# Merging all four token tiles' fetched expert results on VectorE inside the last unit, instead of two on VectorE and two by identity products

## The chip, the core and the metric

One core of one Trainium2 chip runs the whole program. TensorE (PE in the rows) does the matrix products, VectorE (DVE) and ScalarE (ACT) the elementwise work, GpSimd (POOL) a few small operations and the issuing of some transfers, SyncE (SP) the issuing of the weight loads. The metric is the device time of one execution in microseconds; lower is better.

## What is computed

Two trunk layers over 256 context tokens and 256 latent tokens of width 1024. The part that matters here is the seam between the two layers: the mixture of experts of layer 0 ends, its result is added to the stream, and layer 1 begins with its normalisation and its key and value projection. Cut from the reference:

```
comb = jnp.sum(jax.nn.one_hot(global_idx, N_EXPERTS, dtype=F32) * w_exp[..., None], axis=1)
for e in range(N_EXPERTS):
    he = jax.nn.silu(t @ w1[e]) * (t @ w3[e])
    out = out + comb[:, e:e + 1] * (he @ w2[e]).astype(F32)
xl = xl + g2l * hier_moe(hl2, ...)          # the same for the context stream with g2c
...
hl = modulate(rmsnorm(xl, norm1[1]), sh1l, sc1l)      # layer 1 begins
q, k, v = _split(h @ w_qkv, QKV_SPLITS)
```

Each token has two experts. All 512 tokens are four tiles of 128: tiles 0 and 1 are context, 2 and 3 are latent.

## The kernel before

**Units.** Layer 0's experts run as `NU = 12` units (the loop from line 1881, `e` is the place in the order `SEQ`). A unit multiplies its gathered tokens by w1 and w3 (`hidden`), forms `he` = silu times the other product on VectorE (line 1894), turns `he` on TensorE, copies it with ScalarE, and multiplies by w2 into two PSUM banks `py` (lines 1913 to 1928). The first ten units scale `py` and scatter the rows into a memory table `yd`, one half of it for each of a token's two experts. The last two units (`N_LAST = 2`) don't go through memory: ScalarE and VectorE split the scaled `py` into a high part `yh` and a low part `yl` (lines 1947 and 1948, both named `yl` in the rows), and one-hot products with `back` bring them into token order (`to_tokens`, line 1958).

**The fetch.** At the start of unit 10, `get_parts` (line 1859) issues eight loads of 512 KB from GpSimd, two for each tile in the order 0, 1, 2, 3: what the first ten units left in `yd`. Tiles 0 and 1 land in `parts_p` (`pt` in the rows, both of a tile), tiles 2 and 3 in two `d4` tiles each (`ya`, `yb`). The loads can start only when the scatter of unit 9 has landed.

**Two ways into the stream.** `merge(t)` (line 1869) is four VectorE instructions: add the two fetched tiles, multiply by the gate `g2` in two halves, add to the residual `xres`. It runs for tiles 0 and 1, in unit 11, after the products that turn `he`. For tiles 2 and 3, `to_tokens` instead adds the fetched tiles to its PSUM sum by products with the identity: two for each half tile, eight in all (lines 1966 and 1967). After the loop, `finish_half(t, n)` (line 1969) gates the PSUM sum and adds it to `xres` on VectorE and squares on ScalarE; `sums` and `normal` make the normalised tile; `turned` (line 2001) transposes on TensorE; `columns1` (line 2010) applies the modulation on VectorE and splits into two parts; `kv_split` splits the key and value weights.

**What sets the order.** `pin(...)` makes the named engines keep the order of the program text: `m1` from unit 10 on pins TensorE and VectorE, and `fin` (line 2021) pins VectorE, ScalarE and TensorE. So in unit 11 VectorE runs `he`, `merge(0)`, `merge(1)`, then the two `yl`, and an instruction that waits for a load holds all that stand behind it. After the loop TensorE runs `to_tokens` of tiles 0 and 1, one adaLN step (`ada_go`), `to_tokens(2)`, the first transposes `turned((0, 1), 0)`, `to_tokens(3)`, and then the other transposes; the key and value products follow.

**Weights** arrive through SyncE's queue in a ring of slots that the consuming engines free.

Of the kernel before, what the change touches and what calls it, by code (L numbers as in the profile page):

```python
# [27 lines left out]
NU = 12  # L28
# [82 lines left out]
N_LAST = 2  # L111
# [27 lines left out]
def backbone(ctx, tc, I, out):  # L139
    nc = tc.nc  # L140
    act, dve, pool, pe, sp = (Pinned(tc, e) for e in (nc.scalar, nc.vector, nc.gpsimd, nc.tensor, nc.sync))

    def pin(where):
        names = PIN.get(where, "")
        for e, nm in ((act, "a"), (dve, "d"), (pool, "g"), (pe, "p"), (sp, "s")):
            e.on = nm in names
# [11 lines left out]
    def acc():  # L158
        return acc_p.tile([P, 512], F32, tag="acc", name="acc")

    def aux():
        return aux_p.tile([P, 512], F32, tag="aux", name="aux")
# [68 lines left out]
    def feed(key):  # L231
        state["fed"] = where[key]
        pump(state["fed"] + len(slots))
        return loaded.pop(key)
# [125 lines left out]
    ident = const.tile([P, P], F32, name="ident")  # L360
# [193 lines left out]
    def high_if(x):  # L554
        return tc.high_priority() if x else ExitStack()
# [857 lines left out]
    for kk in range(2):  # L1413
        for c in range(4):
            k = 2 * c + kk
# [53 lines left out]
    for n in range(4):  # L1469
        ps = aux()  # L1470
# [6 lines left out]
    for d in range(2):  # L1477
        seq = list(range(8)) if d == 0 else [3, 2, 1, 0, 7, 6, 5, 4]
        for ct in range(2):
            n4 = 2 * d + ct  # L1480
            dsb = [aux(), aux()]
            for c in seq[:-1]:
                pr, t = c % 2, c // 2
# [39 lines left out]
    for tpr in range(2):  # L1523
        at = {}
        for d in range(2):
            ps = [aux(), aux()]
# [25 lines left out]
        ps = [aux(), aux()]  # L1552
        for ti in range(2):
            t = 2 * tpr + ti
            for ct in range(2):
                reg = slice((2 * ti + ct) * P, (2 * ti + ct + 1) * P)
                for pr in range(2):
                    h = 2 * ct + pr
                    for d in range(2 - AT_SUM):
                        pe.matmul(ps[pr][:, reg], at[d, pr][:, reg], vt[:, t, h * P:(h + 1) * P],  # L1560
                                  start=(d == 0), stop=False)
# [8 lines left out]
        for pr in range(2):  # L1570
            o, jk = ob[:, 2 * tpr + pr, :], tmp("jk")
            act.activation(o, ps[pr], AF.Copy)
            for ti in range(2):
                for ct in range(2):
                    reg = slice((2 * ti + ct) * P, (2 * ti + ct + 1) * P)
                    n = (2 * tpr + ti) * 4 + 2 * ct + pr
# [5 lines left out]
    for t in range(4):  # L1582
        for h in range(4):
            n = 4 * t + h
# [24 lines left out]
    for b in range(4):  # L1609
        ps = aux()  # L1610
# [71 lines left out]
    def d4(name):  # L1682
        return wk.tile([P, D], F32, tag="d4", name=name, bufs=N_D4)
# [9 lines left out]
    def fetch_x(i):  # L1693
        if i < NU:
            if i < 2:
                xg = xgs[i] = xg01[:, i * D:(i + 1) * D]
            else:
                xg = xgs[i] = d4("xg")
            if 2 <= i < N_D4:
                pool.memset(xg, 0.0)  # L1700
            gather(0, xg, ix[:, SEQ[i]:SEQ[i] + 1])
# [152 lines left out]
    parts = {}  # L1854
# [14 lines left out]
    def merge(t):  # L1869

        ya, yb = parts[t]
        dve.tensor_tensor(ya, ya, yb, op=ALU.add)
        for n in range(2):
            sl = slice(n * 512, (n + 1) * 512)
            dve.tensor_tensor(ya[:, sl], ya[:, sl], g2[int(t < 2)][n], op=ALU.mult)
        dve.tensor_tensor(xres[:, t, :], xres[:, t, :], ya, op=ALU.add)
# [4 lines left out]
    for e in range(NU):  # L1881
        two = SEQ[e] >= BIG
        if AHEAD > 2:
            fetch_x(e + AHEAD)
        if e == NU - N_LAST:
            pin("m1")
            get_parts()
        sl = wk.tile([P, 512], F32, tag="sl", name="sl")
        act.activation(sl, hs[e, 0], AF.Silu)
        hidden(e, 1, 0)  # L1890
        hidden(e, 1, 1)
        he = wk.tile([P, 4, P], F32, tag="he", name="he")
        with high_if(HE):
            dve.tensor_tensor(he.rearrange("q k p -> q p k"), sl.rearrange("q (p k) -> q p k", k=4),
                              hs[e, 1].rearrange("q (p k) -> q p k", k=4), op=ALU.mult)
        if e + 1 < NU:
            hidden(e + 1, 0, 0)
        ps = aux()
        for k in range(4):
            pe.transpose(ps[:, k * P:(k + 1) * P], he[:, k, :], ident)  # L1900
        hh = wk.tile([P, 512], F32 if two else F32R, tag="hh", name="hf" if two else "hh")
        if not two:
            hl = wk.tile([P, 512], F32R, tag="hl", name="hl")
        with high_if(HE):
            act.activation(hh, ps, AF.Copy)
            if not two:
                dve.tensor_tensor(hl, ps, hh.bitcast(F32), op=ALU.subtract)
        if e + 1 < NU:
            hidden(e + 1, 0, 1)
        if e == NU - 1:  # L1910
            for t in range(2):
                merge(t)
        py = [acc(), acc()]
        for h in range(2):
            if two:
                raws = [feed((2, 0, e, o, h)) for o in range(2)]
                for n in range(2):
                    for kk in range(2):
                        k = 2 * h + kk
                        halves(py[n], hh[:, k * P:(k + 1) * P], raws,  # L1920
                               slice(kk * D + n * 512, kk * D + (n + 1) * 512), k == 0, k == 3)
            else:
                for q, wh, wl in quarters(e, 2, h):
                    k = 2 * h + q
                    ks = slice(k * P, (k + 1) * P)
                    for n in range(2):
                        ws = slice(n * 512, (n + 1) * 512)
                        mm3(py[n], (hh[:, ks], hl[:, ks]), (wh[:, ws], wl[:, ws]), k == 0, k == 3)
            if h == 0 and e + 2 < NU:
                prep_x(e + 2)  # L1930
        if e == NU - LESS:
            less_slots(parts_p)
        if e == 1:
            last_ow = d4("ow")
            for n in range(N_LAST):
                last_tokens(NU - 1 - n)
            A1B1 = ada_cols(1)
        if e == 2:
            for n in range(N_LAST):
                turn_last(NU - 1 - n)  # L1940
        if e == 4:
            g2 = [rows_pe(rowt, i, 2, mod[0], 2) for i in range(2)]
        if e >= NU - N_LAST:
            yh, yl = last_y[e] = [wk.tile([P, D], F32R, tag="d4", name="yl", bufs=N_D4) for _ in range(2)]
            for n in range(2):
                sl = slice(n * 512, (n + 1) * 512)
                act.activation(yh[:, sl], py[n], AF.Copy, scale=wgt[:, SEQ[e]:SEQ[e] + 1])
                dve.scalar_tensor_tensor(yl[:, sl], py[n], wgt[:, SEQ[e]:SEQ[e] + 1], yh[:, sl].bitcast(F32),
                                         op0=ALU.mult, op1=ALU.subtract)
        else:  # L1950
            y = d4("y")
            for n in range(2):
                act.activation(y[:, n * 512:(n + 1) * 512], py[n], AF.Copy, scale=wgt[:, SEQ[e]:SEQ[e] + 1])
            scatter(0, ix[:, NU + SEQ[e]:NU + SEQ[e] + 1], y)
# [3 lines left out]
    def to_tokens(t, n):  # L1958

        sl = slice(n * 512, (n + 1) * 512)  # L1960
        ps = fin[t, n] = (acc, aux)[n]()
        for e in range(NU - N_LAST, NU):
            for k in range(2):
                pe.matmul(ps, back[e - NU][:, t * P:(t + 1) * P], last_y[e][k][:, sl],
                          start=(e + k == NU - N_LAST), stop=(t < 2 and e + k == NU))
        for k in range(2 if t >= 2 else 0):
            pe.matmul(ps, ident, parts[t][k][:, sl], start=False, stop=(k == 1))

    def finish_half(t, n):
        sl = slice(n * 512, (n + 1) * 512)  # L1970
# [30 lines left out]
    def turned(tiles, k2):  # L2001

        ps = aux()
        for k in (k2, k2 + 1):
            for n, t in enumerate(tiles):
                c = 256 * (k - k2) + n * P
                pe.transpose(ps[:, c:c + P], xn[t][:, k * P:(k + 1) * P], ident)
        return ps

    def columns1(s, tiles, k2, ps, v_of):  # L2010

        for k in (k2, k2 + 1):
            v = v_of()
            dve.tensor_scalar(v, ps[:, 256 * (k - k2):256 * (k - k2) + 256], A1[:, k, s:s + 1],
                              B1[:, k, s:s + 1], op0=ALU.mult, op1=ALU.add)
            for n, t in enumerate(tiles):
                hi, lo = (x[t][:, k, :] for x in hs1)
                act.activation(hi, v[:, n * P:(n + 1) * P], AF.Copy)
                dve.tensor_tensor(lo, v[:, n * P:(n + 1) * P], hi.bitcast(F32), op=ALU.subtract)
# [33 lines left out]
    kv_split(0, 0)  # L2053
    ps = [turned((0, 1), 0)]
    v1 = lambda: wk.tile([P, 256], F32, tag="v", name="v", bufs=N_V)
    for n in range(2):
        to_tokens(3, n)
    sums(2, 1)
    for k2 in range(0, KD, 2):
        if k2:  # L2060
            ps.append(turned((0, 1), k2))
        columns1(1, (0, 1), k2, ps.pop(0), v1)
        if k2 < 6:
            kv_split((k2 + 2) // 4, (k2 + 2) // 2 % 2)
        if k2 == 2:
            finish_half(3, 0)
            finish_half(3, 1)
# [403 lines left out]
    for p in range(NE // 2):  # L2471
# [12 lines left out]
        sl, he = (wk.tile([P, 512], F32, tag="y", name=nm, bufs=4) for nm in ("sl", "he"))  # L2484
# [22 lines left out]
        for h in range(2):  # L2507
            raws = [feed((2, 1, 2 * p + o, h)) for o in range(2)]
            for i in range(4):
                n, kk = (i % 2, i // 2) if p >= NE // 2 - KKM else (i // 2, i % 2)  # L2510
                k = 2 * h + kk
# [21 lines left out]
    for n in range(2):  # L2533
        for t in range(2):
            sl = slice(n * 512, (n + 1) * 512)
# [103 lines left out]
```

## Time and profile before

| | us |
|---|---|
| median of 3 executions | 984.44 (983.81 to 985.03) |
| the profiled execution, whole | 992.14 |
| its span | 990.3 |
| TensorE busy in the span | 903.5 (91%) |
| VectorE busy | 528.2 (53%) |
| ScalarE busy | 399.7 (40%) |
| GpSimd busy | 120.8 (12%) |

All stamps below are microseconds from the start of the span of that one profiled execution. TensorE's share is an average over stages with different limits; the seam between the layers lies at about 577 to 645 us. A matmul's end is modelled by the profile, so the starts are what to go by.

### The profile page before, as it was taken

The numbers are of one execution on the slowest core, as the hardware profiler recorded it, in microseconds if no ns is written. First come the engines' busy times: TensorE is split into PE (matmuls) and PEld (weight loads), VectorE is DVE, ScalarE is ACT, GpSimd is POOL, SyncE is SP. The second block draws the span as 40 slices with busy tenths as digits, with TensorE's granted clock in tenths as the row PEclk, the third lists the DMA queues.
The fourth block names the chain that finished last, engine by engine and source line by source line (L and its number), as shares of the span: only waits on it lengthen the run. The fifth ranks groups of instructions, "written<-read, shape, count | busy, mean of one in ns | idle before, by whom it ended". The sixth has DMA issues, their size and how long they took to land. (4 is left out here: it accounts for less than half of the span.)

```text
span 990.3 us, 12557 instructions
## 1 busy us (share of the span) xinstructions
PE 903.5 (91%) x4589; PEld 534.8 (54%) x4589; DVE 528.2 (53%) x992; ACT 399.7 (40%) x693; POOL 120.8 (12%) x130
## 2 busy tenths in 40 slices
PE   5999998999993599989999988999896999999996
PEld 3556455666761556647558635675675344444432
DVE  5496677438577576545539547777646011111112
ACT  4265664044322446637548513465634211111210
POOL 1012431130511311100100200010002000000000
PEclk8999999989996699999999999999997999999999
DMA  9937353559525699999999997856837799999992
GB/s 327 396 141 269 146 199 110 213 182 336 209 94 188 242 397 422 426 424 420 412 425 393 366 425 291 345 213 245 317 106 280 294 422 426 423 424 422 425 422 97
DMA packets 63451, 304.82 MB, mean 308 GB/s; under 512 B 8866, under 2 KB 17698, under 8 KB 35344
## 3 DMA queue, kind: packets, MB, share of 16 engines
q1 hardware_dynamic: 55360, 284.58, 72.7%
q0 software_dynamic: 5120, 14.06, 3.8%
q10 hardware_dynamic: 2896, 5.24, 1.4%
q8 instruction: 39, 0.64, 0.3%
q14 instruction: 36, 0.29, 0.1%
HBM read 295.04 MB, written 12.58 MB: 311 GB/s over the span
## 5 line engine op out<-in xcount | busy, mean ns | idle before, releaser
L131 DVE TENSOR_TENSOR wlo<-raw,whi 128x1024 fp32r<-128x1024 f32 x144 | 175.0, 1233 | 69.0 <-ACT whi L131 64.5
L131 ACT ACTIVATE whi<-raw 128x1024 fp32r<-128x1024 f32 x144 | 150.5, 1059 | 104.8 <-PE acc L131 85.6
L131 PE MATMUL aux<-raw,x 128*64 128x512 f32 x488 | 116.3, 597 | 1.1 <-ACT x L131 0.7
L131 PEld LDWEIGHTS aux<-raw,x 128*64 128x64 f32 x488 | 34.5, 136 | 62.1 <-issue 57.6
L131 PE MATMUL acc<-raw,xf 128*64 128x512 f32 x256 | 59.5, 598 | 1.1 <-DMA raw<-in_w_dram 1.1
L131 PE MATMUL aux<-raw,sl 128*64 128x512 f32 x240 | 57.0, 594 | 0.7 <-ACT sl L131 0.7
L131 PE MATMUL ada<-raw,cT 128*32 128x512 f32 x320 | 52.5, 632 | 0.0
L131 PE MATMUL acc<-whi,xh 128*128 128x512 f32 x128 | 52.3, 409 | 0.0
L131 PE MATMUL acc<-whi,xl 128*128 128x512 f32 x128 | 50.4, 394 | 0.0
L131 PE MATMUL acc<-wlo,xh 128*128 128x512 f32 x128 | 50.4, 394 | 0.0
L131 DVE SCALAR_TENSOR_TENSOR aux<-aux,ws,mod 128x512 f32<-128x512 f32 x8 | 6.1, 759 | 71.6 <-PE aux L131 71.6
L131 PE MATMUL acc<-whi,h 128*128 128x512 f32 x128 | 42.1, 401 | 0.2 <-ACT h L131 0.2
L131 PE MATMUL acc<-hhi,whi 128*128 128x512 f32 x96 | 38.3, 432 | 3.3 <-ACT hhi L131 3.0
L131 PE MATMUL acc<-raw,hf 128*64 128x512 f32 x128 | 34.4, 626 | 4.7 <-DMA raw<-in_w_dram 4.0
L131 DVE TENSOR_TENSOR he<-sl,aux 128x512 f32<-128x512 f32 x8 | 8.4, 1054 | 56.2 <-PE aux L131 56.2
L131 PEld LDWEIGHTS acc<-raw,xf 128*64 128x64 f32 x256 | 18.6, 136 | 34.9 <-issue 30.8
L131 PEld LDWEIGHTS aux<-raw,sl 128*64 128x64 f32 x240 | 17.8, 137 | 35.8 <-issue 33.1
L131 PE MATMUL acc<-hlo,whi 128*128 128x512 f32 x96 | 35.9, 410 | 0.0
L131 POOL DMA_INDIRECT yd<-y,ix x10 | 12.0, 1200 | 191.1 <-ACT y L131 157.8
L131 PE MATMUL acc<-hhi,wlo 128*128 128x512 f32 x96 | 35.0, 400 | 0.0
L131 ACT ACTIVATE x<-gat,B,A 128x256 f32<-128x256 f32 x26 | 13.3, 560 | 41.6 <-PE gat L131 40.8
L131 PE MATMUL acc<-whi,hhi 128*128 128x512 f32 x64 | 27.5, 429 | 1.8 <-ACT v L131 1.8
(454 smaller groups left out, 1806.0 us busy)
## 6 DMA issues: line engine op xcount, KB each, us to landing
raw<-in_w_dram SPq DMA_DIRECT2D x151, 1024.0 KB, 14.5
raw<-in_w_ada_dram SPq DMA_DIRECT2D x38, 1024.0 KB, 5.5
raw<-in_w_dram SPq DMA_DIRECT2D x72, 512.0 KB, 12.2
raw<-in_w_in_dram SPq DMA_DIRECT2D x10, 1024.0 KB, 6.2
raw<-in_w_ada_dram SPq DMA_DIRECT2D x32, 256.0 KB, 6.5
raw<-in_w_qkv_dram SPq DMA_DIRECT2D x6, 1024.0 KB, 15.3
xres<-in_w_dram SPq DMA_DIRECT2D x5, 1024.0 KB, 16.0
raw<-in_w_out_dram SPq DMA_DIRECT2D x4, 1024.0 KB, 6.9
```

The costliest lines, as they stand in the source:

```text
L131: ins = f(*a, **k)
```

## The change

Unit 11 merges all four tiles on VectorE: `merge(0)` ahead of `he`, `merge(1)`, `merge(2)` and `merge(3)` where tiles 0 and 1 were merged. The eight identity products go. `to_tokens(3)` moves from ahead of the loop over columns to behind the second group of transposes.

```diff
@@ in the loop over units, e == 11
         he = wk.tile([P, 4, P], F32, tag="he", name="he")
+        if e == NU - 1:
+            merge(0)
         with high_if(HE):
             dve.tensor_tensor(he..., sl..., hs[e, 1]..., op=ALU.mult)
@@
         if e == NU - 1:
-            for t in range(2):
+            for t in range(1, 4):
                 merge(t)
         py = [acc(), acc()]
@@ to_tokens
                 pe.matmul(ps, back[e - NU][:, t * P:(t + 1) * P], last_y[e][k][:, sl],
-                          start=(e + k == NU - N_LAST), stop=(t < 2 and e + k == NU))
-        for k in range(2 if t >= 2 else 0):
-            pe.matmul(ps, ident, parts[t][k][:, sl], start=False, stop=(k == 1))
+                          start=(e + k == NU - N_LAST), stop=(e + k == NU))
@@ after the loop
-    for n in range(2):
-        to_tokens(3, n)
     sums(2, 1)
     for k2 in range(0, KD, 2):
         if k2:
             ps.append(turned((0, 1), k2))
+        if k2 == 2:
+            for n in range(2):
+                to_tokens(3, n)
         columns1(1, (0, 1), k2, ps.pop(0), v1)
```

## Rows read from the trace of the kernel before

**Rows 1.** Stretches: from:to, length, busy (instructions) of each engine, granted clock, DMA.
```profile
592.00:605.00 13.00, 10.35 (x42) 5.90 (x42) 11.20 (x26) 5.43 (x14) 1.11 (x2) 0.99 1.02 428
605.00:645.00 40.00, 38.80 (x175) 25.64 (x175) 28.98 (x76) 17.06 (x52) 1.79 (x3) 0.96 0.71 278
```
**Rows 2.** VectorE in order of time, unit 11: start, length, operation, [idle before <-what ended it].
```profile
577.42 1.03 DVE L131 TENSOR_TENSOR he<-sl,acc 128x512 f32<-128x512 f32 x1 [5.58 <-PE acc L131]
...
584.10 1.23 DVE L131 TENSOR_TENSOR pt<-pt 128x1024 f32<-128x1024 f32 x1 [2.01 <-DMA pt<-yd]
585.36 1.29 DVE L131 TENSOR_TENSOR pt<-pt,row 128x512 f32<-128x512 f32 x2
586.69 1.23 DVE L131 TENSOR_TENSOR xres<-xres,pt 128x1024 f32<-128x1024 f32 x1
589.67 0.75 DVE L131 SCALAR_TENSOR_TENSOR yl<-acc,wgt,yl 128x512 fp32r<-128x512 f32 x1 [1.76 <-ACT yl L131]
...
593.22 0.68 DVE L131 TENSOR_TENSOR jk<-acc,row 128x512 f32<-128x512 f32 x1
```
**Rows 3.** Issues of the fetch on GpSimd, one of SyncE: start, length, what.
```profile
563.59 0.60 POOL L131 DMA_DIRECT2D pt<-yd  x1 [8.22 <-DMA yd<-y,ix]
564.19 1.10 POOL L131 DMA_DIRECT2D pt<-yd  x2
565.28 0.54 POOL L131 DMA_DIRECT2D pt<-yd  x1
567.39 0.54 POOL L131 DMA_DIRECT2D yb<-yd  x1
583.94 7.05 SPq L131 DMA_DIRECT2D raw<-in_w_qkv_dram  x2
```
**Rows 4.** Issues in windows of one or two: KB each, median us from issue to landing.
```profile
pt<-yd POOLq DMA_DIRECT2D x1, 512.0 KB, 9.4
pt<-yd POOLq DMA_DIRECT2D x2, 512.0 KB, 10.9
pt<-yd POOLq DMA_DIRECT2D x1, 512.0 KB, 18.7
yb<-yd POOLq DMA_DIRECT2D x1, 512.0 KB, 31.4
raw<-in_w_qkv_dram SPq DMA_DIRECT2D x1, 1024.0 KB, 18.4
```
**Rows 5.** DMA queues from 568 to 598: packets, MB, share of 16 engines.
```profile
q1 hardware_dynamic: 1183, 8.63, 68.1%
q0 software_dynamic: 1130, 4.11, 33.5%
```
**Rows 6.** TensorE in order of time around the identity products and the first transposes.
```profile
591.73 1.19 PE L131 MATMUL acc<-yl,back 128*128 128x512 f32 x4
597.63 1.02 PE L131 MATMUL acc<-ya,ident 128*128 128x512 f32 x2
604.91 0.90 PE L131 MATMUL aux<-ident,pt 128*128 128x128 f32 x3 [2.65 <-DVE ssq L131]
605.46 2.06 PE L131 MATMUL acc<-yl,back 128*128 128x512 f32 x4
612.12 1.04 PE L131 MATMUL aux<-ident,pt 128*128 128x128 f32 x8
```
**Rows 7.** VectorE's waits for TensorE behind the identity products.
```profile
602.19 0.69 DVE L131 TENSOR_TENSOR jk<-aux,row 128x512 f32<-128x512 f32 x1 [0.74 <-PE aux L131]
612.75 0.54 DVE L131 TENSOR_SCALAR v<-aux,A,B 128x256 f32<-128x256 f32 x1 [1.24 <-PE aux L131]
```
**Rows 8.** Stretches around the longest idle time of TensorE, columns as in rows 1.
```profile
758.00:760.00 2.00, 0.00 (x0) 0.00 (x0) 2.00 (x3) 1.59 (x3) 2.00 (x2) 0.50 1.03 436
762.00:764.00 2.00, 1.28 (x6) 1.28 (x7) 1.83 (x13) 0.20 (x1) 0.00 (x0) 0.50 0.40 168
766.00:768.00 2.00, 2.00 (x11) 1.92 (x9) 0.00 (x0) 1.09 (x3) 0.00 (x0) 0.50 0.03 8
```

## Prediction

> **What bounds the kernel now.** I began with the share of busy time, but it is an average; the change lives at the seam between the two layers, so I read the stretches there. Up to 605 us the DMA engines are full (share 1.02, 428 GB/s), TensorE and VectorE each have some idle time; from 605 to 645 TensorE is busy 38.8 of 40 us and VectorE 29.0 [rows 1]. Then I read VectorE in order of time. It waits for the last products of unit 11, runs `he` at 577.42, then `merge(0)` and `merge(1)`, the latter after a wait of 2.01 us for a load, then waits for ScalarE and forms the first `yl` at 589.67; its first `finish_half` starts at 593.22 [rows 2]. From there to the key and value products its chain runs nearly without holes; the two holes that TensorE makes are 0.74 us at 602.19 (`to_tokens(2)` with its identity products) and 1.24 us at 612.75 (`to_tokens(3)`) [rows 7]. In the view of TensorE the identity products start at 597.63, and `to_tokens(3)` lies between 605.46 and 612.12 [rows 6]. Last I read what nobody waited for in the old order, the landings of the fetch: the eight loads are issued between 563.59 and 567.39 [rows 3] but land one after the other [rows 4].
>
> **When the fetched tiles are there.** The first load lands 9.4 us after its issue, at 573.0. The window with the first two has a middle value of 10.9, so the second took 12.4 and lands at 564.19 + 12.4 = 576.6: tile 0 is complete. The fourth: 565.28 + 18.7 = 584.0, and VectorE's wait for tile 1 ends at 584.10, so stamps and landings agree within 0.1 us. The eighth: 567.39 + 31.4 = 598.8: tile 3 is complete only then [rows 2 to 4]. The last four are thus 14.8 us behind the fourth, 3.7 us for each 512 KB. They are slow because they share the DMA engines with SyncE's weight loads: between 568 and 598 GpSimd's queue moved 4.11 MB and SyncE's 8.63 MB, in 1130 and 1183 packets [rows 5].
>
> The Trainium skill ("DMA: Bandwidth & Descriptors", section Queues, rings and completion order) says that each DMA engine takes turns between the queues that have work, a packet at a time. The packets counted here agree with that: as many of one as of the other, and the bytes go one to two because GpSimd's are half as large. It speaks against the change as long as SyncE's queue has work; its other side, that GpSimd's loads speed up where that queue runs dry, is the second rival below.
>
> **The change, part by part.**
>
> *merge(0) ahead of `he`.* A merge takes VectorE from 584.10 to 587.92, 3.8 us [rows 2]. With tile 0 complete at 576.6 it runs from 576.7 to 580.5, and `he` starts there instead of at 577.42: 3.1 us later. Behind it wait TensorE's turn of `he`, ScalarE's copy and the w2 products. In the old order TensorE is through with them 14.3 us after the start of `he` (591.73 against 577.42 [rows 2, 6]), so now at about 594.8. I cost this at nothing, because the next wait ends later; without that cover it is 3.1 us.
>
> *merge(1) to merge(3) ahead of the two `yl`.* This adds the wait that counts. VectorE takes its instructions in the order of the text, pinned in unit 11. `merge(3)` can't start before 598.8 and ends at 598.9 + 3.8 = 602.7; the two `yl` follow (0.75 us each), and the first `finish_half` starts at 604.2 instead of 593.22 [rows 2]. **That is 11.0 us late.** TensorE waits for the same `yl` in its first `to_tokens`, with all of `to_tokens`, the adaLN step and the transposes behind it; ScalarE's squares and GpSimd's small powers wait for `finish_half`; SyncE's next loads wait for slots that the key and value splits free. The merges' own 7.6 us of extra VectorE time lies inside this wait and is not added.
>
> *The clock after the stall.* TensorE is idle from about 595 to 603. What it does then is not in the trace of before; the nearest row is its longest idle time: nothing in 758 to 760, then busy again from about 762, and the granted clock is 0.50 (1.2 GHz) during the idle time and still in 766 to 768 [rows 8]. At that level the four products of a half tile take 1.86 us from start to start (605.46 to the next group at 607.32, the same level), against 1.4 us that VectorE needs for one `finish_half` (0.68 us for the first of its two long instructions and as much for the second). So each of six halves may wait 0.5 us: bounds 0 and 3.0, and I take 1.5, since the low clock of rows 8 lasts for some of these halves, not for all.
>
> *The identity products go.* For tile 2 that frees VectorE from its wait of 0.74 us [rows 7]; nothing else is late there, VectorE's chain is. For tile 3 the bounds are VectorE's wait of 1.24 us [rows 7] and what TensorE saves: 6.7 us (605.46 to 612.12) less some 2 us for the products that stay, 4.7 [rows 6]. TensorE is nearly full to 645 [rows 1], which speaks for more than the lower bound; the transposes of each next pair of columns are fed by VectorE, which speaks for little more. I take 2.0.
>
> *`to_tokens(3)` behind the second transposes* is what makes that possible: the second transposes no longer stand behind it. Its result is wanted by `finish_half(3, ·)` only after the second group of columns, so the move costs nothing; if VectorE were already there, it would cost the 2 us of its products.
>
> **The sum.** 11.0 + 1.5 − 0.7 − 2.0 = +9.8 us. The rest of the program hangs on the key and value products, so I let it pass to the end. The profiled execution took 992.14 us, 1.8 of them outside the span of 990.3; by the sum the changed one takes 1001.9. The median of the runs is 984.44, 7.7 below the profiled one; the same difference gives **994.2 us**. With all bounds: 11.0 + 0 − 0.7 − 4.7 = +5.6 to 11.0 + 3.0 − 0.7 − 1.2 = +12.1.
>
> **The rivals.**
>
> *The loads land in time (not slower).* The place is the last landing. VectorE's first `finish_half` starts 5.4 us after it; with 2.7 us saved behind it the change breaks even when tile 3 is complete at 593.22 − 5.4 + 2.7 = 590.5, that is 8.3 us earlier than in the trace. Were the 4.19 MB carried at half of 428 GB/s, they would take 19.6 us instead of the eight times 3.7 us = 29.6, counted from 569.3, and land at 588.9: 588.9 + 5.4 − 593.22 − 2.7 = −1.6, so **982.8**; with TensorE's whole 4.7 us, 980.1. For it: the runs without a profile are 0.8% shorter, and I can't see their landings. Against it: the split between the queues is seen over 30 us, and nothing ahead of the fetch changes.
>
> *SyncE's queue runs dry while TensorE stalls.* Then GpSimd's rest would get the whole 428 GB/s from 594.8 on: at 3.7 us for 512 KB some 0.57 MB are left, 1.3 us of transfer, and the last landing is at 596.1. That is 2.7 us less: +7.1, **991.5**. Against it: a weight load issued at 583.94 takes 18.4 us and lands at 602.3 [rows 3, 4], so the queue has work beyond 598.8.
>
> *The order is not as the text has it*: the merges of tiles 2 and 3 come only behind the two `yl`, or between the `finish_half`. At the latest sensible place, ahead of `finish_half(2, 0)`, their 7.6 us lie on VectorE's chain, less the 2.7 saved: +4.9, **989.3**. Against it: both engines are pinned here, and in the trace of before the order is that of the text [rows 2].
>
> *More than the sum*: the low clock covers all halves and the delay of `he` pushes TensorE past `merge(3)`: +12.1 and more, some **997**.
>
> **How the numbers follow.** Forecast, tile 3's landing decides (+8 to +11.5): 0.65. Same with more saved, SyncE dry, or another order (+3.5 to +8): 0.18. Above +11.5: 0.08. Loads in time: 0.09, of which 0.05 faster by over 0.2% and 0.04 within. About 0.2%, 2 us, is what a measurement of this kernel can tell from no change. Faster 0.05, same 0.04, slower 0.91. The range 988.0 to 997.0 takes in the sum's bounds (990.0 to 996.5), the dry queue and most of the other order, and leaves out the in-time case and what lies beyond.
>
> **What would show it.** In the trace of the changed kernel: VectorE idle before the first instruction of `merge(3)`, ended by a load, at about 599; idle before `merge(0)` to 576.7 and `he` at 580.5; the first `yl` at about 602.7; TensorE idle some 8 us before the last products of the first `to_tokens`; no wait for TensorE at the second group of columns. It is wrong if `yl` starts within a few us of 590, if the last fetched tile lands before 591, or if the delay at the first `finish_half` is there but is given back before the key and value products end.

## Result and the profile after

The changed kernel takes 996.4 us (median of 4, 992.5 to 997.3) against 984.5 us: ratio 1.0113 with a 95% interval of 1.0089 to 1.0137, **11.9 us slower**. Run again beside the other kernels below it gave 1.0120 (1.0092 to 1.0148), 998.0 against 985.1 us. The runs of both kernels spread over some us, so single times are not compared below, only ratios with intervals and stages of traces.

All stamps of the changed kernel below are from its profiled execution of 995.92 us. It reaches the seam 3.84 us earlier than the first profile of before did (last hidden products of unit 11 at 566.42 against 570.26), since executions differ by some us in earlier stages that the change doesn't touch (these products start between 561.06 and 570.74 us in the profiles of this case). So stages are compared by their distance from those products, called **zero** here.

VectorE in order of time, unit 11 and behind it, as in [rows 2]:

```profile
572.53 1.23 DVE L131 TENSOR_TENSOR pt<-pt 128x1024 f32<-128x1024 f32 x1 [4.53 <-DMA pt<-yd]
...
576.25 1.02 DVE L131 TENSOR_TENSOR he<-sl,acc 128x512 f32<-128x512 f32 x1
579.91 1.23 DVE L131 TENSOR_TENSOR pt<-pt 128x1024 f32<-128x1024 f32 x1 [2.64 <-DMA pt<-yd]
...
587.30 1.23 DVE L131 TENSOR_TENSOR ya<-ya,yb 128x1024 f32<-128x1024 f32 x1 [3.58 <-DMA yb<-yd]
...
594.68 1.23 DVE L131 TENSOR_TENSOR ya<-ya,yb 128x1024 f32<-128x1024 f32 x1 [3.56 <-DMA yb<-yd]
...
598.41 1.40 DVE L131 SCALAR_TENSOR_TENSOR yl<-acc,wgt,yl 128x512 fp32r<-128x512 f32 x2
600.04 0.69 DVE L131 TENSOR_TENSOR jk<-acc,row 128x512 f32<-128x512 f32 x1 [0.23 <-PE acc L131]
...
601.75 0.69 DVE L131 TENSOR_TENSOR jk<-aux,row 128x512 f32<-128x512 f32 x1 [0.29 <-PE aux L131]
...
634.53 0.75 DVE L131 TENSOR_SCALAR xn<-xres,r 128x1024 f32<-128x1024 f32 x1
```

Each of the four merges begins with idle time that a load ends. The two `yl` stand behind the last of them and start at 598.41, 31.99 us from zero; in [rows 2] the first was at 19.4. The last row makes the last normalised tile, the end of the seam in what follows, 68.1 us from zero. What TensorE does meanwhile, from zero on:

```profile
566.42 7.09 PE L131 MATMUL acc<-raw,xf 128*64 128x512 f32 x32
577.33 0.66 PE L131 MATMUL aux<-ident,he 128*128 128x128 f32 x4 [3.83 <-DVE he L131]
578.67 8.50 PE L131 MATMUL acc<-raw,hf 128*64 128x512 f32 x32 [0.69 <-ACT hf L131]
587.10 0.96 PE L131 MATMUL acc<-yl,back 128*128 128x512 f32 x3
599.21 0.79 PE L131 MATMUL acc<-yl,back 128*128 128x512 f32 x1 [11.15 <-DVE yl L131]
...
611.28 1.75 PE L131 MATMUL aux<-ident,pt 128*128 128x128 f32 x7 [3.64 <-DVE ssq L131]
612.69 2.06 PE L131 MATMUL acc<-yl,back 128*128 128x512 f32 x4
614.54 1.62 PE L131 MATMUL aux<-yl,back 128*128 128x512 f32 x4
```

It is done with unit 11 at about 588 and waits 11.15 us for `yl`, in the middle of the first `to_tokens`. The landing of the eighth load, the queues while the eight are under way (563.7 to 594) and then from TensorE's stall to the last landing (588 to 594.6), and the clock in stretches of 2 us (columns as in [rows 1]):

```profile
yb<-yd POOLq DMA_DIRECT2D x1, 512.0 KB, 31.0
```
```profile
q1 hardware_dynamic: 1188, 8.66, 67.7%
q0 software_dynamic: 1147, 4.18, 33.8%
```
```profile
q1 hardware_dynamic: 288, 2.10, 75.2%
q0 software_dynamic: 210, 0.73, 27.1%
```
```profile
594.00:596.00 2.00, 0.00 (x0) 0.00 (x0) 1.29 (x2) 0.00 (x0) 0.00 (x0) 0.50 1.02 430
...
600.00:602.00 2.00, 2.00 (x7) 1.52 (x6) 1.64 (x3) 0.45 (x1) 0.00 (x0) 0.50 0.57 242
602.00:604.00 2.00, 2.00 (x12) 1.27 (x14) 1.93 (x5) 1.00 (x4) 0.00 (x0) 0.99 0.11 45
...
612.00:614.00 2.00, 2.00 (x8) 1.81 (x7) 1.76 (x5) 0.44 (x2) 0.55 (x1) 0.50 0.00 0
```

The load took 31.0 us, as before (31.4 in [rows 4]), with the same share between the queues as in [rows 5]; the DMA engines were full until the last of them had landed. The low clock behind the long wait lasted into 600 to 602. A second spell followed TensorE's wait of 3.64 us: the granted clock was 0.50 in 612 to 614, where `to_tokens(3)` ran (2.06 and 1.62 us), but VectorE waited for none of it.

### The profile page after: what moved, and what is told of

Same layout as the page of the kernel before. It is cut to its first block, busy times and chain, and to the rows that moved or that the text cites. A ratio compares the mean times of both kernels' runs of the same rounds, so it can differ in the third digit from the quotient of the medians.

```text
span 994.2 us, 12530 instructions
## 1 busy us (share of the span) xinstructions
PE 892.7 (90%) x4573; PEld 530.1 (53%) x4573; DVE 535.3 (54%) x1000; ACT 400.0 (40%) x693; POOL 120.8 (12%) x130
## 5 line engine op out<-in xcount | busy, mean ns | idle before, releaser
L131 PEld LDWEIGHTS aux<-raw,x 128*64 128x64 f32 x488 | 34.5, 137 | 62.2 <-issue 58.0
L131 PE MATMUL acc<-raw,xf 128*64 128x512 f32 x256 | 59.4, 597 | 0.8 <-DMA raw<-in_w_dram 0.8
L131 PEld LDWEIGHTS acc<-raw,xf 128*64 128x64 f32 x256 | 18.4, 136 | 34.8 <-issue 32.3
L131 PEld LDWEIGHTS acc<-whi,h 128*128 128x128 f32 x128 | 24.0, 188 | 10.7 <-ACT h L131 4.6
```

The source lines that it names most:

```text
L131: ins = f(*a, **k)
```

## Experiments

### A second profile of the kernel before

> The kernel before once more, for a profile from the same chip as the next three. The profiled execution of before that stands ahead of the prediction took 7.7 us more than the median of its runs. Both theories expect a time near 984.5 us; the profile should show at which stage those 7.7 us lay, so that the seam of the changed kernel is set against the right trace. If the seam (from the last hidden products of unit 11 to the key and value products) has the same length as in the first profile, the 7.7 us lie elsewhere.

989.2 us in this one execution. VectorE from the last `he` on, then TensorE's last hidden products (zero) and its second group of w2 products, then that group in the first profile of before:

```profile
577.90 1.03 DVE L131 TENSOR_TENSOR he<-sl,acc 128x512 f32<-128x512 f32 x1 [5.58 <-PE acc L131]
...
589.16 0.75 DVE L131 SCALAR_TENSOR_TENSOR yl<-acc,wgt,yl 128x512 fp32r<-128x512 f32 x1 [0.49 <-ACT yl L131]
...
591.55 0.68 DVE L131 TENSOR_TENSOR jk<-acc,row 128x512 f32<-128x512 f32 x1
...
600.53 0.69 DVE L131 TENSOR_TENSOR jk<-aux,row 128x512 f32<-128x512 f32 x1 [0.76 <-PE aux L131]
...
609.78 0.54 DVE L131 TENSOR_SCALAR v<-aux,A,B 128x256 f32<-128x256 f32 x1
...
626.52 0.75 DVE L131 TENSOR_SCALAR xn<-xres,r 128x1024 f32<-128x1024 f32 x1
```
```profile
570.74 7.09 PE L131 MATMUL acc<-raw,xf 128*64 128x512 f32 x32
...
586.47 3.65 PE L131 MATMUL acc<-raw,hf 128*64 128x512 f32 x14 [1.64 <-DMA raw<-in_w_dram]
```
```profile
586.45 5.34 PE L131 MATMUL acc<-raw,hf 128*64 128x512 f32 x14 [2.10 <-DMA raw<-in_w_dram]
```

Zero is 570.74 here. The first `finish_half` starts 20.8 us from zero, not 22.96; the last normalised tile is made at 55.8, not 59.2. So the seam itself was 3.4 us longer in the first profile. Up to the first `finish_half` it lost 2.15 us: unit 11 waited 2.10 us for weights instead of 1.64 and then ran its last products in 5.34 us instead of 3.65 (granted clock 0.50 in 588 to 590, against 1.00 in the second profile). `to_tokens(3)` ran at the low clock too (0.50 in 606 to 608), which made VectorE's wait of 1.24 us [rows 7]. Here that wait doesn't exist (609.78 has no idle time before it). Two more profiles of kernels whose work up to the first `finish_half` is that of before (`move_only` and `ada_late_move`, below) have it at 21.4 and 21.7 us. The first profile, on which the prediction rests, is the latest of the four. The experiments are set against the second; since profiles of before itself end the seam between 55.8 and 59.2, a difference of 3 us in one profile is not shown by that alone.

| kernel | `he` | first `yl` | first `finish_half` | last normalised tile | against before_again | ratio of times |
|---|---|---|---|---|---|---|
| before_again | 7.2 | 18.4 | 20.8 | 55.8 | | |
| change | 9.8 | 32.0 | 33.6 | 68.1 | +12.3 | 1.0113 (1.0089 to 1.0137) |
| after_again | 9.5 | 31.6 | 33.3 | 68.4 | +12.6 | 1.0120 (1.0092 to 1.0148) |
| t3_reads_t2 | 10.1 | 28.7 | 30.3 | 64.8 | +9.0 | 1.0083 (1.0055 to 1.0112) |
| t23_reads_t01 | 10.2 | 25.0 | 26.4 | 60.5 | +4.7 | 1.0047 (1.0025 to 1.0070) |
| late23 | 10.5 | 21.0 | 23.4 | 64.9 | +9.1 | 1.0105 (1.0064 to 1.0147) |
| m0_only | 10.5 | 21.4 | 23.8 | 58.8 | +3.0 | 1.0024 (1.0006 to 1.0043) |
| after_m0_old | 7.2 | 32.4 | 34.1 | 68.6 | +12.8 | 1.0098 (1.0069 to 1.0127) |

The stamps are starts in us from zero; one per mille of the time is 0.985 us.

### The wait for tile 3 taken away, then that for tile 2 too

```diff
 def merge(t):
-        ya, yb = parts[t]
+        ya, yb = parts[min(t, 2)]        # t3_reads_t2
+        ya, yb = parts[t % 2]            # t23_reads_t01
```

> The changed kernel, but merge(3) reads the fetched tiles of tile 2 a second time instead of its own (the loads are all still issued). So tile 3 of the output is not the reference's. Theory landing: the first yl waits for the last landing that a merge ahead of it reads. That is now tile 2's, awaited in the trace of the changed kernel until 587.30; merge(2) and merge(3) run back to back, 7.6 us, and yl starts at 594.9 instead of 598.41: 3.5 us less, about 992.9 us. Theory order and work: what costs is four merges ahead of yl and the low clock, so nothing changes: 996.4 us.

> The changed kernel, but merge(2) and merge(3) read the fetched tiles of tiles 0 and 1 again (the loads are all still issued), so tiles 2 and 3 of the output are not the reference's. Theory landing: VectorE waits only for tile 1 (to 579.91 in the trace of the changed kernel), then runs three merges without a hole, 11.4 us, and yl starts at 591.3 instead of 598.41; 7.1 us less, about 989.3 us, and before the key and value products only the 3.8 us that the merges stick out and the savings remain, so +1 to +5 against the kernel before. Theory order and work: the same 996.4 us as the change.

The two kernels in that order, VectorE's second and third of the waits and its `yl`:

```profile
586.40 1.22 DVE L131 TENSOR_TENSOR ya<-ya,yb 128x1024 f32<-128x1024 f32 x1 [3.59 <-DMA yb<-yd]
...
590.25 1.22 DVE L131 TENSOR_TENSOR ya<-ya,yb 128x1024 f32<-128x1024 f32 x1
...
593.98 1.40 DVE L131 SCALAR_TENSOR_TENSOR yl<-acc,wgt,yl 128x512 fp32r<-128x512 f32 x2
```
```profile
578.55 1.23 DVE L131 TENSOR_TENSOR pt<-pt 128x1024 f32<-128x1024 f32 x1 [2.58 <-DMA pt<-yd]
...
582.28 1.22 DVE L131 TENSOR_TENSOR pt<-pt 128x1024 f32<-128x1024 f32 x1
...
586.01 1.22 DVE L131 TENSOR_TENSOR pt<-pt 128x1024 f32<-128x1024 f32 x1
...
589.73 1.40 DVE L131 SCALAR_TENSOR_TENSOR yl<-acc,wgt,yl 128x512 fp32r<-128x512 f32 x2
```

With the same instructions, only other data, `yl` moves 3.3 and 7.0 us ahead, and the last normalised tile 3.3 and 7.6 us; the times go the same way (3.0 and 6.5 us by the ratios; the interval of the first overlaps that of the change, that of the second doesn't). This is the landing theory's answer, and the other one (nothing changes) is out. The second kernel also shows what is left with no late landing at all: tile 1's, at 578.55, is still followed by 11.2 us of merges, so `yl` is 6.6 us later than in before_again and the end of the seam 4.7 us. Of the change's 12.3 us at the seam, 7.6 are thus the two late landings (with the short waits for TensorE behind them); the other 4.7 are merges that don't fit between tile 1's landing and `yl`, less what the identity products give back.

### The two late merges behind `yl`

```diff
-            for t in range(1, 4):
-                merge(t)
+            merge(1)
 ...
+    merge(2)
     finish_half(2, 0)
 ...
+            merge(3)
             finish_half(3, 0)
```

> The changed kernel with merge(2) moved to just ahead of finish_half(2, 0) and merge(3) to just ahead of finish_half(3, 0): all the work of the change, none of the two late waits ahead of yl. Theory landing: both tiles have long landed where they are read, yl starts 10 us earlier than in the change, and the 7.6 us of the two merges lie on VectorE's chain, less 2.7 us that the identity products cost before: +4.9 against before, 989.4 us; if the key and value products hide part of merge(3), less. Theory order and work: as slow as the change, 996 us.

A miss of 5 us: 994.8 us, and by the time alone what the theory of order and work said. Its VectorE:

```profile
588.32 0.75 DVE L131 SCALAR_TENSOR_TENSOR yl<-acc,wgt,yl 128x512 fp32r<-128x512 f32 x1 [3.06 <-ACT yl L131]
...
597.48 1.22 DVE L131 TENSOR_TENSOR ya<-ya,yb 128x1024 f32<-128x1024 f32 x1
...
616.37 1.22 DVE L131 TENSOR_TENSOR ya<-ya,yb 128x1024 f32<-128x1024 f32 x1
```

The waits are gone: `yl` starts at 21.0 us from zero, and neither merge waits for anything. But 7.4 us of merges (597.48 to 601.20 and 616.37 to 620.09) lie on VectorE's chain, the first `finish_half` is 2.6 us late because of `he`, and from there to the last normalised tile it takes 41.5 us against 35.0 in before_again, so only 0.9 us comes back where identity products stood: 2.6 + 7.4 − 0.9 = 9.1, the +9.1 of the table. I had credited 2.7 us for the identity products and nothing for `he`. So the landing theory was right that the waits go and wrong on what is left without them. In the change the work of the two late merges hides inside the waits for their loads; here the waits are gone and the same work lies open on VectorE's chain. That is 3.2 us better than the change at the seam, and by the ratios the two can't be told apart.

### merge(0) ahead of `he`, alone and taken back

```diff
+        if e == NU - 1:
+            merge(0)                      # m0_only: in the kernel before
         with high_if(HE): ...
-            for t in range(2):
-                merge(t)
+            merge(1)
```

> The kernel before with one part of the change: merge(0) ahead of he; merge(1) where it was, tiles 2 and 3 by identity products. Theory chain: he waits for tile 0's landing and the merge, 2.6 us as in the traces of the change and of late23, and nothing hides it, because the w2 products, yl and finish_half follow on one chain: +2.6 us. Theory cover (as the prediction costed it, at nothing): the wait of the w2 products for weights (2.1 and 1.6 us in the two profiles of before) takes its place: 0 to +1 us.

```diff
-        if e == NU - 1:
-            merge(0)                      # after_m0_old: in the changed kernel
 ...
-            for t in range(1, 4):
+            for t in range(4):
```

> The changed kernel with merge(0) back behind he, so that all four merges stand between he and yl. This tests the step of the prediction that costed the delay of he at nothing because the wait for tile 3 ends later. Theory landing: yl still starts 3.9 us after tile 3's landing, so the time is that of the change, 996 to 998 us, although merge(0) ahead of he alone cost 2.4 us in the kernel before. Rival: the two delays add, and it is 2.4 us less than the change, 994 us.

By the ratio m0_only costs 2.4 us (0.6 to 4.2), by the seam 3.0. The interval alone leaves room for both theories; the rows of m0_only tell more (TensorE, and a stretch with columns as in [rows 1]):

```profile
572.59 1.11 PE L131 MATMUL aux<-ident,he 128*128 128x128 f32 x4 [4.44 <-DVE he L131]
574.38 9.04 PE L131 MATMUL acc<-raw,hf 128*64 128x512 f32 x32 [0.69 <-ACT hf L131]
```
```profile
576.00:578.00 2.00, 2.00 (x8) 0.62 (x6) 1.93 (x4) 0.00 (x0) 0.00 (x0) 0.50 1.03 430
```

`he` is 3.3 us late here (10.5 against 7.2), and 3.0 of it reach the first `finish_half`. The wait for weights is gone, as theory cover said. But TensorE, after 4.44 us without work, runs the first w2 products at a granted clock of 0.50 (1.2 GHz), so that from `he` to the first product with `back` it still needs 11.9 us against 12.2 in before_again: hardly anything is hidden. In the changed kernel, taking `merge(0)` back behind `he` brings `he` to 7.2 us from zero, but `yl` stays at 32.4:

```profile
572.47 1.03 DVE L131 TENSOR_TENSOR he<-sl,acc 128x512 f32<-128x512 f32 x1 [5.58 <-PE acc L131]
...
593.98 1.23 DVE L131 TENSOR_TENSOR ya<-ya,yb 128x1024 f32<-128x1024 f32 x1 [3.55 <-DMA yb<-yd]
...
597.71 1.40 DVE L131 SCALAR_TENSOR_TENSOR yl<-acc,wgt,yl 128x512 fp32r<-128x512 f32 x2
```

So there the wait for tile 3 does cover it, as the seam shows. The times don't decide between the two theories: 995.0 us lies between 994 and 996, and the ratios of the two kernels (1.0098 and 1.0120) have overlapping intervals.

### to_tokens(3) moved, alone

```diff
-    for n in range(2):
-        to_tokens(3, n)
 ...
         if k2:
             ps.append(turned((0, 1), k2))
+        if k2 == 2:
+            for n in range(2):
+                to_tokens(3, n)
```

> The kernel before with one part of the change: to_tokens(3), identity products included, moved behind the second transposes. The prediction read a wait of 1.24 us of VectorE at the second group of columns in the first profile of before; the second profile of before has none there, since TensorE ran to_tokens(3) at the full clock. Theory chain: VectorE bounds this stretch, so no difference, within 1 us. Theory TensorE: up to 1.2 us less.

The identity products are kept in it. Ratio 0.9996 (0.9975 to 1.0017), and from the first `finish_half` to the last normalised tile it takes 35.0 us as in before_again: no difference.

### Candidates to beat both

All three also have `to_tokens(3)` behind the second transposes, as in `move_only`; the first cut leaves that out.

```diff
             for t in range(2):
                 merge(t)
+            for t in (2, 3):
+                pool.tensor_tensor(parts[t][0], parts[t][0], parts[t][1], op=ALU.add)
 ...
-        for k in range(2 if t >= 2 else 0):
-            pe.matmul(ps, ident, parts[t][k][:, sl], start=False, stop=(k == 1))
+        if t >= 2:
+            pe.matmul(ps, ident, parts[t][0][:, sl], start=False, stop=True)
```

> A candidate: GpSimd, idle here, adds the two fetched tiles of tiles 2 and 3 in memory as they land, and to_tokens adds the sum by one identity product instead of two; to_tokens(3) behind the second transposes. No wait ahead of yl is added. Theory chain: only VectorE's wait of 0.76 us in finish_half(2, 1) goes: -0.8 us against before. Theory TensorE: half of the identity time of 6.9 us comes back, -2 to -3 us. If GpSimd's sum of tile 2 is not ready when to_tokens(2) wants it (about 7 us after the first yl), TensorE waits and it is slower by that.

Slower: 1.0030 (1.0012 to 1.0048). VectorE, then GpSimd:

```profile
588.68 0.69 DVE L131 TENSOR_TENSOR jk<-aux,row 128x512 f32<-128x512 f32 x1
589.40 2.16 DVE L131 TENSOR_TENSOR xres<-xres,jk 128x512 f32<-128x512 f32 x1
...
598.36 0.16 DVE L131 TENSOR_TENSOR rs_t<-r 128x1 f32<-128x1 f32 x1 [3.95 <-POOL r L131]
```
```profile
588.10 2.91 POOL L131 TENSOR_TENSOR ya<-ya,yb 128x1024 f32<-128x1024 f32 x1 [23.56 <-DMA yb<-yd]
595.47 2.34 POOL L131 TENSOR_TENSOR ya<-ya,yb 128x1024 f32<-128x1024 f32 x1 [4.45 <-DMA yb<-yd]
597.76 0.56 POOL L131 TENSOR_TENSOR r<-ssq,half_neg 128x1 f32<-128x1 f32 x1
```

The mistake of the change again, on GpSimd: the addition for tile 3 waits for its load, and the small power `r` that `normal(0)` needs stands behind it; VectorE waits 3.95 us. In the next one that addition stands behind the powers, just ahead of `to_tokens(3)`:

```diff
-            for t in (2, 3):
-                pool.tensor_tensor(parts[t][0], parts[t][0], parts[t][1], op=ALU.add)
+            pool.tensor_tensor(parts[2][0], parts[2][0], parts[2][1], op=ALU.add)
 ...
         if k2 == 2:
+            tc.keep_in_program_order(nc.gpsimd.tensor_tensor(parts[3][0], parts[3][0], parts[3][1], op=ALU.add))
             for n in range(2):
                 to_tokens(3, n)
```

> The candidate with GpSimd's additions, the one of tile 3 now behind the small powers that normal() waits for (in the first candidate it stood ahead of them, waited for tile 3's load, and normal(0) waited 3.95 us for GpSimd). Theory chain: that wait is gone, and what is left is VectorE's wait of 0.76 us that no longer exists, against two VectorE instructions that took 1.5 us longer while GpSimd added (2.16 instead of 0.69 us): 0 to +2 us against before. Theory TensorE: the saved identity products count, -2 us.

1.0036 (1.0016 to 1.0056), still slower, by 3.6 us at the seam (last normalised tile at 59.4 us from zero). Of these, 0.9 us lie ahead of the first `finish_half`, as in ada_late_move, which has no addition on GpSimd. The 3.95 us are gone, but VectorE was held up during both additions, by 1.5 and 2.1 us, and only the wait of 0.76 us is saved; here the second, VectorE's row and then GpSimd's:

```profile
601.32 2.30 DVE L131 TENSOR_TENSOR rs_t<-r 128x1 f32<-128x1 f32 x1 [0.21 <-POOL r L131]
```
```profile
601.25 2.35 POOL L2062 TENSOR_TENSOR ya<-ya,yb 128x1024 f32<-128x1024 f32 x1
```

The last candidate changes only TensorE's order, the cut being what it has beyond `move_only`:

```diff
-    ada_go(KA0)
     for n in range(2):
         to_tokens(2, n)
+    ada_go(KA0)
```

> A second candidate, no arithmetic changed: the kernel before with to_tokens(3) behind the second transposes and the adaLN step (1 us of TensorE) behind to_tokens(2) instead of ahead of it, so that finish_half(2, 1) need not wait for TensorE. Theory chain: VectorE's wait of 0.76 us goes: -0.8 us, hardly more than can be measured. Rival: the adaLN step frees a slot of the weight ring later, the next load of key and value weights lands later, and it is the same or slower by up to 2 us.

Ratio 0.9989 (0.9967 to 1.0010): VectorE no longer waits in `finish_half(2, 1)`, and from the first `finish_half` to the last normalised tile it takes 34.1 us instead of 35.0, but in the time the gain is below what can be measured. No version beat the kernel before.

## Why the prediction was right, step by step

It gave 994.2 us, 988 to 997, slower at 0.91; measured 996.4, and the place and the mechanism are the ones it named.

- **Landings.** Right: the eighth load took 31.0 us, VectorE's wait before `merge(3)` ended with it, and the wait was the last one ahead of `yl`. By moving which landing is read, the experiments show that the late landings cause 7.6 of the 12.3 us. The rest is not the landing: three merges behind tile 1 take longer than unit 11 leaves room for, which the prediction did not price.
- **`merge(0)` ahead of `he`.** 3.1 us forecast, 2.7 seen. Costing it at nothing was right inside the change (after_m0_old), and only there: alone it costs 2.4 us. TensorE came to its products with `back` 10.9 us after `he`, not 14.3, since the old figure held the wait for weights; so it waited 11.15 us for `yl` where some 8 were forecast.
- **The delay of the first `finish_half`.** 11.0 us forecast; 12.8 us against the second profile of before, 10.7 against the first. Against its own profile the term was right within 0.3 us. It was small against the second because the first profile's unit 11 had lost 2.15 us itself, to the longer wait for weights and to the low clock behind it.
- **The clock.** 1.5 us taken, from rows at another place of the program; here VectorE waited 0.23 and 0.29 us for slow products, the first of them ahead of the first `finish_half`. In after_again there were four such waits, 0.96 us in all, so the size varies between executions; both profiles stay below the 1.5.
- **Identity products.** 2.0 + 0.7 us taken. From the first `finish_half` to the last normalised tile the change needs 34.5 us against 35.0 of the second profile of before, with 0.3 us of slow products in it: 0.8 saved, not 2.7. That is the term for tile 2 (the wait of 0.76 us at 600.53 is gone); the 2.0 for tile 3 gave nothing. The step that failed is the reading of VectorE's wait at 612.75 [rows 7] as a cost of `to_tokens(3)`; it came from the low clock of that one execution, and move_only shows no gain from the move. In the change `to_tokens(3)` ran at the low clock too and nobody waited, so in an execution with such a spell the move may spare the 1.24 us; that was not tested. Saving 6.9 us of TensorE's time (eight times 0.86 us in before_again) returns little where VectorE's chain bounds the stage.
- **The sum.** 12.8 + 0.3 − 0.8 = +12.3, as the seam shows, against +9.8. Against the first profile the seam grew by 8.9. So the sum was 0.9 too high for the execution it was worked out on and 2.5 too low for the second one. The errors partly cancelled, and that the time came within 2.2 us is in part luck: the +9.8 was reckoned from the first profile's long seam, but put onto the median of the runs.
- **All of it passes to the end.** In the main: against the second profile of before, 11.1 us are left at the end of the trace of the change, and 15.2 at the end of after_again's. Behind the last normalised tile the two profiles of the change need 359.7 and 363.5 us, four of before's order (both profiles of before, move_only, ada_late_move) 360.8 to 361.1. What makes executions differ there was not tested; nothing shows that a part of the delay is regularly given back.
- **The rivals.** *Loads in time*: its condition, tile 3 complete 8 us earlier, was not met; its price was wrong, since t23_reads_t01, which waits for neither late tile, is still 4.7 us slower: the rival forgot that three merges in a row take longer than unit 11 leaves room for. *SyncE dry*: not seen. While TensorE stalled (588 to 594.6), SyncE's queue still moved 2.10 MB against GpSimd's 0.73, and tile 3 came 7.4 us behind tile 2, the 3.7 us for each load that were forecast. *Another order*: the order was that of the text; the other would have cost 9.1, not 4.9 (late23). *More than the sum*: its time, some 997, is close to what was measured, but neither of its conditions was met: TensorE was done with unit 11 at 588, before `merge(3)` began at 594.68, and the low clock cost 0.3 us.

## What to carry to other kernels

Before work is put on an engine that takes its instructions in order, look up when its inputs land, even if nobody waits for them yet: a load that was free because its reader came late becomes the bound when its reader is moved ahead of the critical evacuation. Products that add into an accumulation later in the order can read late data without holding anything up; here they read tile 3 from 607.32 on in the first profile of before, 8.5 us after it landed. Read a stage from more than one profile before a wait in it is booked as a cost; a single one can hold another execution's stall.

## What was not expected of the hardware

While GpSimd added two 128x1024 tiles, VectorE's instructions with two operands in SBUF, the on-chip memory, lasted until GpSimd was done: one of 0.69 us took 2.16 us (589.40 to 591.56, where GpSimd's addition, from 588.10, ended at 591.01), and one of 0.16 us took 2.30 (to 603.62, GpSimd's to 603.60). One with an operand in PSUM, TensorE's accumulator (`aux`, 588.68), took its 0.69 us beside the first addition. The Trainium skill ("SBUF — State Buffer", section SBUF: two separate sides) says that the two engines take a shared pair of ports in turn for whole instructions, VectorE's with two inputs in SBUF included; the rows agree. In pool_add_late it took back 3.6 us, more than the 0.8 us that the shorter `to_tokens` gave.
